# Twenty of forty-eight gate projections moved into a stage of their own, with seven block products for eight

## The chip, the cores and the metric

The kernel runs on one core of a Trainium2 chip. The metric is device time in microseconds (us) of one execution. Three executions of the kernel before took 2284.29 us in the median (2282.69 to 2284.61). On this core TensorE (PE in the profile) multiplies matrices, VectorE (DVE), ScalarE (ACT) and GpSimd (POOL) do everything else, and SyncE (SP) issues every DMA of this kernel. Each engine takes its instructions in the order written for it and waits at the first one whose operands aren't ready.

## The reference

One decoder layer on 1024 tokens of width 1024. Only its first part matters here:

```
proj = x @ w_in + b_in                     # 1024 x 8200
ml_qk, ml_v, ml_o, ml_if, da_q, da_k, da_v, gates = split(proj)
q, k = split(silu(causal_dwconv(ml_qk)))   # 4 heads of 128
h    = head_layer_norm(mlstm_chunkwise(q, k, ml_v, ...))
y_a  = (sigmoid(ml_o) * h) @ w_proj_a
o    = head_rms_norm(diff_attention(rope(da_q), rope(da_k), da_v))   # 8 heads
y_b  = o @ w_proj_b
g_a, g_b = split(sigmoid(gates))           # 1024 each
x = layer_norm(alpha * x + (g_a * y_a + g_b * y_b) @ w_mix_out)
```

After it come cross-attention into 256 memory tokens (its keys and values don't depend on x) and a SwiGLU feed-forward part. The columns `ml_o` (1024, eight blocks of 128) and `gates` (2048, sixteen blocks) are the 24 gate projections this case is about; with the blocks of `ml_qk`, `da_q` and `da_k` there are 48 blocks in `wfm`.

## The kernel before, in words

Every projection is done in float32 accuracy as three matmuls on split operands: a value is held as a rounded high part and a remainder (`whi`/`wlo` for weights, `bh`/`bl` for the input x, `to_hi` and `to_lo`), and `mm3` (L151 to L152) adds hi*hi, hi*lo and lo*hi in PSUM. The high part of a weight is made by ScalarE and GpSimd in turn (L139, L141), the remainder by VectorE three times of four and by GpSimd the fourth (L149).

`g_fm` (L191) projects one block of 128 columns: 8 blocks of 128 input channels by two halves of 512 tokens, so 2 x 8 x 3 = 48 matmuls of 128x512. It yields after every `mm3` by three matmuls; such a step is called a quantum here. `Weave` holds a queue of such generators. The mixers yield a number, and the driver then takes so many quanta from the queue (`W.pump(n)`); what is left is drained at fixed places. PE's order is therefore the order in which the program is written out. The order on the other engines is set by a scheduler, with priorities raised for loads and splits of weights.

The stages, by time in the profile:

1. **kv stage** (0 to 59 us): 16 blocks of cross-attention keys and values (`g_kv`, matmuls of 128x256). Beside them `g_x` loads the eight slabs of x and splits them into `xT`, which stays until the end of attention.
2. **mLSTM** (59 to about 455 us): first `g_first` (values and gate logits), then the projections `q`, `k` and two `o` blocks of head 0. For each of four heads `mlstm(h)` then pumps 68 quanta of the queue between its own small matmuls. The queue holds the next head's v, q, k and two `o` blocks (32 + 16 + 16 + 16 + 16 quanta), and five gate blocks in the last head. What isn't pumped is drained before the next head. `mlstm` starts with `PE.transpose` of k (L440), ends with transposes of the normalized h (L501). k comes from `g_proj_qk` (L350 to L369): evacuation on ACT (L356), a causal convolution on DVE (L359, L361), tanh on ACT (L367), a scale on POOL (L368) and a product on DVE (L369).
3. **Attention** (455 to about 1100 us): eight heads. Before head 0 `addB(0)` projects V, Q and K; each head pumps 64 quanta. `FILL` says what a head's queue holds: `P` is the next head's Q, K (16 quanta each) and, for every second head, V for two heads (32), `G` a gate block (16), `q`/`v` products of cross-attention weights (8 each). `scores` makes the probabilities (DVE, ACT, POOL), `values` transposes them (L719, L722), splits them and multiplies by V. `Y` are the first products after attention; they need `hT`, which `h0` to `h3` load into the memory of `xT`.
4. **Merge, cross-attention, feed-forward** (1100 to 2283 us). Gates kept in DRAM (`g_d`) are read again by `gate` (L827). The feed-forward part multiplies 2x2 blocks with seven products for eight (`g_seven`).

Of the kernel before, what the change touches and what calls it, by code (L numbers as in the profile page):

```python
# [115 lines left out]
def hybrid_layer(ctx: ExitStack, tc: tile.TileContext, a: dict, out: bass.AP):  # L116
# [74 lines left out]
    def g_fm(wsrc, acts, evac, pool=None, w=None):  # L191

        w = w or split_all(load_w(wsrc, pool), 1024, pool)
# [48 lines left out]
    g_d = dr.tile([16, 128, 1024], F, name="g_d")  # L242
    row_d = dr.tile([2, 32, 128], F, name="row_d")
# [3 lines left out]
    xT = big4(xp, "big", 4)  # L247
    with tc.tile_pool(name="mp", bufs=1, reuse_waits="tile") as mp:
# [11 lines left out]
        def g_x(k):  # L260
            load_slab(xT, k, a["xT"][:, k, :])
            yield from ()
# [15 lines left out]
        for k in range(0, 8, 2):  # L278
            if k % 4 == 0:
                turn["plan"] = ("v", "v")  # L280
                first.append(split_w(w0[:, k * 128:k * 128 + 512], mp))
# [16 lines left out]
    ngate = cst.tile([128, 16], F, name="ngate")  # L298
    V.tensor_scalar(ngate, bfm[:, 32:48], -1.0, None, op0=OP.mult)
# [6 lines left out]
    V.memset(pio2, math.pi / 2)  # L306

# [25 lines left out]
    with tc.tile_pool(name="ap", bufs=1, reuse_waits="tile") as A:  # L333
        ltbig = A.tile([128, 128], F, name="ltbig")
        dma(ltbig, a["c_ltbig"])
        bhalf = A.tile([128, 48], F, name="bhalf")
        V.tensor_scalar(bhalf, bfm, 0.5, None, op0=OP.mult)
# [75 lines left out]
        def g_gate(i, pool, tag, bufs):  # L413
            def ev(j, acc):
                gt = pool.tile([128, 512], F, tag=tag, name="gt", bufs=bufs)
                if i < NG_A:
                    res["act2"] = S.activation(gt, acc, AF.Tanh, scale=0.5, bias=bhalf[:, 32 + i:33 + i]).ins
                elif i < 8:
                    S.activation(gt, acc, AF.Exp, scale=-1.0, bias=ngate[:, i:i + 1])
                else:  # L420
                    S.activation(gt, acc, AF.Identity, bias=bfm[:, 32 + i:33 + i])
                dma(g_d[i][:, j * 512:(j + 1) * 512], gt)
# [88 lines left out]
        def addA(h):  # L511
# [3 lines left out]
            for d in range(2):  # L515
                W.add(f"o{h}{d}", g_proj_o(h, d))
# [76 lines left out]
        for h in range(4):  # L593
# [11 lines left out]
    with tc.tile_pool(name="bp", bufs=1, reuse_waits="tile") as B:  # L605
# [187 lines left out]

        gates = iter(range(NG_A, 16))

# [32 lines left out]
        def gate(i, pool, tag):  # L828
            gt = pool.tile([128, 1024], F, tag=tag, name="gt", bufs=2)
            dma(gt, g_d[i])  # L830
            if NG_A <= i < 8:
                S.activation(gt, gt, AF.Ln, bias=1.0)
                S.activation(gt, gt, AF.Exp, scale=-1.0)
                return gt
            if i >= 8:
                S.activation(gt, gt, AF.Tanh, scale=0.5)
# [11 lines left out]
        def add_fill(nm, h):  # L848
            if nm == "G":
                W.add("g", g_gate(next(gates), B, "rope", NROPE))  # L850
            elif nm == "P":
# [11 lines left out]
        add_fill("G", 0)  # L863
# [565 lines left out]
```

## Time and profile before

| | |
|---|---|
| median of three executions | 2284.29 us |
| profiled execution, its own time | 2285.06 us |
| its span (first to last instruction) | 2283.3 us |
| PE busy | 2207.3 us, 97% of the span |
| PE weight loads (PEld) | 2008.0 us, 88% |
| DVE / ACT / POOL busy | 1421.2 / 696.4 / 704.9 us |
| mean granted clock of PE | 0.989 of full speed |

PE's busy time in the profile comes from modelled ends: matmuls overlap, so one that follows another starts 0.227 us after it (128x512) though it is shown 0.39 us long. What PE really does is read from the starts and from the idle time in front of an instruction, with the engine that ended it.

### The profile page before, as it was taken

Reading aid. Unit: us, or ns where it says so; the run is one execution under the profiler, and the core shown is the slowest. Engines: PE = TensorE matmul, PEld = TensorE weight load, DVE = VectorE, ACT = ScalarE, POOL = GpSimd, SP = SyncE. Lnnn points to the kernel's source line nnn. Section 1 sums busy time; section 2 is a strip of 40 time slices with the busy share of each in tenths; the row PEclk is TensorE's granted clock in tenths of the full one; section 3 lists DMA queues with packets and bytes.
Section 4 is the critical chain, followed back from the end, with each engine's and each line's share of the span. In section 5 each row is a group of like instructions: output and inputs, shape, how many; then the busy total and the mean of one; then the engine's idle time right before and its main releaser. Section 6 shows DMA issues by size and latency. Waiting matters only on the chain.

```text
span 2283.3 us, 36224 instructions
## 1 busy us (share of the span) xinstructions
PE 2207.3 (97%) x14109; PEld 2008.0 (88%) x14109; DVE 1421.2 (62%) x2655; ACT 696.4 (30%) x1375; POOL 704.9 (31%) x720
## 2 busy tenths in 40 slices
PE   8999999999999999998999999997999999999997
PEld 8898898887988888886888999997899999999996
DVE  8536645357777676676535486478756665556657
ACT  3322213234454454445232123222211111111122
POOL 7124323233333332334412232245421111111124
PEclk9999999999999999999999999999999999999999
DMA  8322222344263343439733423222211111111122
GB/s 319 102 73 93 83 65 88 127 124 132 63 181 100 81 128 83 108 103 316 254 137 138 177 83 105 81 84 74 65 39 54 47 46 56 56 48 45 56 64 94
DMA packets 97963, 238.47 MB, mean 104 GB/s; under 512 B 12128, under 2 KB 30464, under 8 KB 97792
## 3 DMA queue, kind: packets, MB, share of 16 engines
q1 hardware_dynamic: 97792, 236.16, 32.5%
q8 instruction: 111, 1.82, 0.3%
q14 instruction: 60, 0.49, 0.1%
HBM read 168.92 MB, written 41.98 MB: 92 GB/s over the span
## 4 chain that ended last, share of the span: by engine, by line
PE 51%; DVE 5%; DMA 2%; issue 2%; POOL 1%; ACT 1%; SPq 0%; DVEq 0%; POOLq 0%; ACTq 0%
PE acc L152 32%; PE xb L152 7%; PE xa L152 5%; PE xc L152 5%; DVE wlo L149 1%; DMA vo_d<-ev 1%; PE sp L152 1%; DVE d L1040 1%; PE op L152 1%; DVE z L930 0%; DVE xb L149 0%; PE tp L722 0%; DVE z L926 0%; DVE u L1040 0%; PE tp L1007 0%
## 5 line engine op out<-in xcount | busy, mean ns | idle before, releaser
L141 POOL TENSOR_SCALAR whi<-wraw 128x512 fp32r<-128x512 f32 (+1 forms) x250 | 180.0, 720 | 880.3 <-issue 355.6
L152 PE MATMUL acc<-bh,whi 128*128 128x512 f32 x1024 | 418.1, 408 | 0.4 <-ACT gtok L389 0.4
L149 DVE TENSOR_TENSOR wlo<-wraw,whi 128x512 fp32r<-128x512 f32 (+1 forms) x379 | 306.3, 813 | 160.8 <-ACT whi L139 121.1
L152 PE MATMUL acc<-bh,wlo 128*128 128x512 f32 x1024 | 402.2, 393 | 0.0
L152 PE MATMUL acc<-bl,whi 128*128 128x512 f32 x1024 | 402.0, 393 | 0.0
L139 ACT ACTIVATE whi<-wraw 128x512 fp32r<-128x512 f32 (+1 forms) x252 | 157.4, 626 | 550.9 <-PE acc L152 273.9
L152 PEld LDWEIGHTS acc<-bh,wlo 128*128 128x128 f32 x1024 | 193.6, 189 | 42.5
L152 PEld LDWEIGHTS acc<-bh,whi 128*128 128x128 f32 x1024 | 194.0, 189 | 33.4 <-ACT gtok L389 0.6
L152 PEld LDWEIGHTS acc<-bl,whi 128*128 128x128 f32 x1024 | 194.3, 190 | 32.3
L152 PE MATMUL acc<-whi,bh 128*128 128x256 f32 (+1 forms) x728 | 213.2, 293 | 0.2 <-DVE ev L149 0.2
L152 PE MATMUL acc<-whi,bl 128*128 128x256 f32 (+1 forms) x728 | 205.6, 282 | 0.0
L152 PE MATMUL acc<-wlo,bh 128*128 128x256 f32 (+1 forms) x728 | 205.4, 282 | 0.0
L152 PE MATMUL xb<-xe,whi 128*128 128x256 f32 x1008 | 183.8, 283 | 10.3 <-DVE u L1040 7.4
L149 POOL TENSOR_TENSOR wlo<-wraw,whi 128x512 fp32r<-128x512 f32 (+1 forms) x125 | 174.1, 1393 | 9.8
L152 PEld LDWEIGHTS xb<-xe,whi 128*128 128x128 f32 x1008 | 155.9, 190 | 10.9 <-issue 6.8
L152 PE MATMUL xb<-xe,wlo 128*128 128x256 f32 x504 | 142.5, 283 | 0.0
L152 PEld LDWEIGHTS acc<-whi,bh 128*128 128x128 f32 x728 | 138.7, 190 | 2.0 <-DVE ev L149 0.4
L152 PEld LDWEIGHTS acc<-wlo,bh 128*128 128x128 f32 x728 | 138.7, 190 | 1.6
L152 PEld LDWEIGHTS acc<-whi,bl 128*128 128x128 f32 x728 | 138.6, 190 | 0.0
L1250 DVE SCALAR_TENSOR_TENSOR z<-z,acc 128x512 f32<-128x512 f32 x144 | 98.2, 685 | 53.4 <-PE acc L152 51.8
L152 PE MATMUL xa<-xb,whi 128*128 128x256 f32 x672 | 125.5, 287 | 5.2 <-ACT u L1162 5.2
L152 PE MATMUL acc<-wlo,hidh 128*128 128x512 f32 x320 | 124.7, 390 | 1.4 <-DVE wlo L149 1.4
(315 smaller groups left out, 5205.1 us busy)
## 6 DMA issues: line engine op xcount, KB each, us to landing
wraw<-in_wfm_dram SPq DMA_DIRECT2D x48, 512.0 KB, 3.6
wraw<-in_wg_dram SPq DMA_DIRECT2D x24, 512.0 KB, 3.6
wraw<-in_wu_dram SPq DMA_DIRECT2D x24, 512.0 KB, 3.5
wraw<-in_wd_dram SPq DMA_DIRECT2D x22, 512.0 KB, 3.5
hT_d<-hp SPq DMA_DIRECT2D x16, 512.0 KB, 2.8
g_d<-gt SPq DMA_DIRECT2D x32, 256.0 KB, 2.3
K<-rot SPq DMA_DIRECT2D x64, 128.0 KB, 2.3
klo<-raw SPq DMA_DIRECT2D x64, 128.0 KB, 2.3
```

Of the source, the lines that this page charges most:

```text
L139: S.activation(dst, src, AF.Copy)
L141: G.tensor_scalar(dst, src, 1.0, 0.0, op0=OP.mult, op1=OP.add)
L149: (V if eng == "v" else G).tensor_tensor(dst, src, hi.bitcast(F), op=OP.subtract)
L152: PE.matmul(o, l, r, start=start, stop=stop, skip_group_check=True)
L1040: V.tensor_tensor(dst, x_, y_, op=op)
L1250: V.scalar_tensor_tensor(zs, zs, ALPHA if q == 0 else 1.0, acc, op0=OP.mult, op1=OP.add)
```

## The change

Eight `o` blocks and twelve of sixteen gate blocks leave the mixers' queues. They are computed in pairs, in a stage of their own between the kv stage and the mLSTM. A pair of blocks (2 x 128 columns) is seen as a 2x2 matrix of blocks, x as well; sums of the blocks are formed, and seven products of 12 matmuls (128x512) and five additions out of PSUM give what eight products gave. The sums of x (`xs`, four more split tiles) are formed in the kv stage by `g_x`, which now takes two slabs at a time. tanh is applied at once; the results go to DRAM (`o_d`, `g_d`), and `g_o` loads a block of `o_d` where a head's `o` was projected. The last mLSTM head keeps four gate blocks. In attention the `G` entries are gone and the products of cross-attention weights are spread otherwise. In the kv stage weights are split into the general pool (4 buffers instead of 6) and three raw buffers stand for four.

```diff
-X_AT = (3, 4, 6, 7, 9, 10, 12, 13)
+X_AT = (3, 6, 9, 12)
-NRAW = 4
+NRAW = 3
-NG_A = 5
-FILL = (("G", "q0", "P", "G"), ("P", "q1"), ("G", "q2", "P", "G"), ("P", "G"), ("G", "q3", "P", "G"), ("P", "G"),
-        ("G", "P", "G"), ("h0", "v0", "h1", "v1", "h2", "v2", "h3", "v3", "Y"))
+NG_A = 4
+FILL = (("q0", "P", "q1"), ("P",), ("q2", "P", "q3"), ("P",), ("v0", "P", "v1"), ("P",), ("v2", "P", "v3"),
+        ("h0", "h1", "h2", "h3", "Y"))
...
         def g_x(k):
-            load_slab(xT, k, a["xT"][:, k, :])
+            raw = [load_w(a["xT"][:, kk, :]) for kk in (k, k + 4)]
+            b11, b12, b21, b22 = (r[:, hs] for r in raw for hs in HALVES)
+            for kk, r in zip((k, k + 4), raw):
+                for h, hs in enumerate(HALVES):
+                    to_hi(xT[h][0][:, kk, :], r[:, hs], "s")
+                    to_lo(xT[h][1][:, kk, :], r[:, hs], xT[h][0][:, kk, :], "v")
+            def put_(n, src):
+                to_hi(xs[n][0][:, k, :], src, "s")
+                to_lo(xs[n][1][:, k, :], src, xs[n][0][:, k, :], "g")
+            V.tensor_tensor(b11, b12, b11, op=OP.subtract)
+            put_(0, b11)
+            V.tensor_tensor(b12, b22, b12, op=OP.subtract)
+            put_(2, b12)
+            V.tensor_tensor(b22, b22, b11, op=OP.subtract)
+            put_(1, b22)
+            V.tensor_tensor(b21, b21, b22, op=OP.subtract)
+            put_(3, b21)
...
+        def g_dense(t0, t1, evac):
+            w = sums7([load_w(a["wfm"][t_]) for t_ in (t0, t1)])
+            def prod(bank, b, start=False, stop=False):
+                for k in range(4):
+                    mm3(bank, cut(w[b], k * 128, k * 128 + 128), (xblk[b][0][k], xblk[b][1][k]),
+                        start and k == 0, stop and k == 3)
+                    yield
...
+        for h in range(4):
+            W.add("o", g_sig(8 + 2 * h, o_d[2 * h:2 * h + 2]))
+        for i in range(0, 16 - NG_A, 2):
+            W.add("g", g_sig(32 + i, g_d[i:i + 2]))
+        W.drain()
...
-        def g_proj_o(h, d):
-            t_ = 8 + h * 2 + d
+        def g_o(h, d):
             og = A.tile([128, 1024], F, tag="og", name="og", bufs=3)
-            def ev(j, acc):
-                res["act2"] = S.activation(og[:, j * 512:(j + 1) * 512], acc, AF.Tanh, scale=0.5,
-                                           bias=bhalf[:, t_:t_ + 1]).ins
-            yield from g_fm(a["wfm"][t_], xT, ev)
+            dma(og, o_d[2 * h + d])
             G.tensor_scalar(og, og, 0.5, 0.5, op0=OP.mult, op1=OP.add)
...
             else:
-                for i in range(NG_A):
-                    W.add(f"g{i}", g_gate(i, A, "th", 2))
+                for i in range(16 - NG_A, 16):
+                    W.add(f"g{i}", g_gate(i))
...
         addB(0)
-        add_fill("G", 0)
         W.drain()
```

On PE, at the end of an mLSTM head before, the third transposes of h (`sm<-ident,hn`) follow the last matmul of the next head's k, and the `o` projections (`acc<-bh,whi` and so on) come behind them:

```order
L152 MATMUL acc<-bh,whi 128x512
L152 MATMUL acc<-bl,whi 128x512
L152 MATMUL acc<-bh,wlo 128x512
L501 MATMUL sm<-ident,hn 128x128 x4
L152 MATMUL acc<-bh,whi 128x512
L152 MATMUL acc<-bl,whi 128x512
L152 MATMUL acc<-bh,wlo 128x512
```

In all 96 such matmuls stand between the last matmul of k and the transposes of that k (`sm<-ident,y`). On PE at the same place of the changed kernel:

```order
L152 MATMUL acc<-bl,whi 128x512
L152 MATMUL acc<-bh,wlo 128x512
L598 MATMUL sm<-ident,hn 128x128 x8
L537 MATMUL sm<-ident,y 128x128 x4
L152 MATMUL acc<-whi,bh 128x256
L152 MATMUL acc<-wlo,bh 128x256
```

The first two rows are the end of k's projection; only eight transposes of h now stand between it and the transposes of k.

On POOL, at the start of the kv stage before (`whi`/`wlo` are weights, `bh`/`bl` are x):

```order
L141 TENSOR_SCALAR whi<-wraw 128x512 x2
L149 TENSOR_TENSOR wlo<-wraw,whi 128x512
L141 TENSOR_SCALAR whi<-wraw 128x512
L141 TENSOR_SCALAR bh<-wraw 128x512
L149 TENSOR_TENSOR bl<-wraw,bh 128x512
L141 TENSOR_SCALAR whi<-wraw 128x512
L141 TENSOR_SCALAR bh<-wraw 128x512
```

And on POOL at the same place of the changed kernel (`t0l` to `t3l` are remainders of the sums of x):

```order
L141 TENSOR_SCALAR whi<-wraw 128x512
L149 TENSOR_TENSOR t0l<-wraw,t0h 128x512
L149 TENSOR_TENSOR t2l<-wraw,t2h 128x512
L141 TENSOR_SCALAR whi<-wraw 128x512
L149 TENSOR_TENSOR t1l<-wraw,t1h 128x512
L149 TENSOR_TENSOR wlo<-wraw,whi 128x512
L149 TENSOR_TENSOR t3l<-wraw,t3h 128x512
```

The high parts of x left POOL for ACT, and 16 subtractions for the sums came; DVE got the 4 remainders of x that POOL had, and 16 subtractions of blocks.

On PE, at the end of attention head 0 before, the last group of `values` alternates transposes of probabilities (`tp`) with quanta (`acc`):

```order
L152 MATMUL op<-ath,vl 128x128
L152 MATMUL acc<-bh,whi 128x512
L152 MATMUL acc<-bl,whi 128x512
L152 MATMUL acc<-bh,wlo 128x512
L152 MATMUL acc<-bh,whi 128x512
L152 MATMUL acc<-bl,whi 128x512
L152 MATMUL acc<-bh,wlo 128x512
L722 MATMUL tp<-ident,e_4941 128x128
L722 MATMUL tp<-ident,e_4990 128x128
```

On PE at the same place of the changed kernel, where the queue of head 0 has run out:

```order
L152 MATMUL op<-ath,vl 128x128
L819 MATMUL tp<-ident,e_5832 128x128
L819 MATMUL tp<-ident,e_5881 128x128
L819 MATMUL tp<-ident,e_5832 128x128
L819 MATMUL tp<-ident,e_5881 128x128
L819 MATMUL tp<-ident,e_5832 128x128
```

The quanta are gone from the last group of heads 0, 2, 4 and 6, whose queues hold 48 quanta for the 64 that are pumped.

## Rows read from the trace of the kernel before

**Rows 1.** The page: busy time, share and instructions of the engines.

```profile
PE 2207.3 (97%) x14109; PEld 2008.0 (88%) x14109; DVE 1421.2 (62%) x2655; ACT 696.4 (30%) x1375; POOL 704.9 (31%) x720
```

**Rows 2.** Windows by stage: length, PE, PEld, DVE, ACT, POOL, PEclk, DMA, GB/s.

```profile
10.00:55.00 45.00, 43.52 (x349) 42.84 (x349) 44.40 (x52) 17.68 (x37) 42.72 (x37) 1.00 0.96 346
125.00:450.00 325.00, 325.00 (x1833) 284.69 (x1832) 158.07 (x269) 86.56 (x186) 98.59 (x85) 1.00 0.26 88
500.00:1050.00 550.00, 524.82 (x3052) 461.03 (x3051) 391.92 (x973) 260.75 (x567) 193.72 (x210) 0.98 0.41 114
1050.00:1075.00 25.00, 17.21 (x69) 13.18 (x68) 14.46 (x33) 10.79 (x21) 8.22 (x9) 0.86 0.99 351
```

**Rows 3.** Chain of waits, a run of 128x512 matmuls: start, length, what.

```profile
1649.48 21.82 PE acc L152 x96
```

**Rows 4.** Groups by form, 10 to 55 us: busy, mean ns | idle before.

```profile
L149 DVE TENSOR_TENSOR wlo<-wraw,whi 128x512 fp32r<-128x512 f32 x23 | 25.2, 1126 | 0.0
...
L141 POOL TENSOR_SCALAR whi<-wraw 128x512 fp32r<-128x512 f32 x15 | 14.9, 998 | 10.9 <-DMA wraw<-in_wxk_dram 10.9
L149 DVE TENSOR_TENSOR bl<-wraw,bh 128x512 fp32r<-128x512 f32 x12 | 14.7, 1235 | 0.5 <-POOL bh L141 0.5
L149 POOL TENSOR_TENSOR wlo<-wraw,whi 128x512 fp32r<-128x512 f32 x7 | 11.3, 1620 | 0.6
...
L149 DVE TENSOR_TENSOR ev<-acc,ev 128x256 fp32r<-128x256 f32 x14 | 5.8, 413 | 0.1
```

**Rows 5.** Timeline of DVE before POOL begins: start, length, instruction.

```profile
3.79 0.69 DVE L149 TENSOR_TENSOR wlo<-wraw,whi 128x512 fp32r<-128x512 f32 x1
```

**Rows 6.** Timeline of PE at the end of mLSTM head 0.

```profile
186.11 0.60 PE L501 MATMUL sm<-ident,hn 128*128 128x128 f32 x4
...
208.82 0.60 PE L440 MATMUL sm<-ident,y 128*128 128x128 f32 x4
```

**Rows 7.** Timeline of ACT at the same place.

```profile
190.89 0.67 ACT L356 ACTIVATE pad<-acc,bfm 128x512 f32<-128x512 f32 x1
196.27 0.63 ACT L139 ACTIVATE hp<-hs 128x512 fp32r<-128x512 f32 x1 [4.71 <-DMA hT_d<-hp]
...
201.08 1.15 ACT L367 ACTIVATE th<-y 128x512 f32<-128x512 f32 x2 [0.31 <-DVE y L361]
```

**Rows 8.** Timeline of POOL at the same place.

```profile
192.04 3.03 POOL L149 TENSOR_TENSOR hp<-hs,hp 128x512 fp32r<-128x512 f32 x2
...
202.19 1.20 POOL L368 TENSOR_SCALAR th<-th 128x512 f32<-128x512 f32 x2
```

**Rows 9.** Timeline of DVE at the same place.

```profile
196.21 4.84 DVE L361 SCALAR_TENSOR_TENSOR y<-pad,cw,y 128x1024 f32<-128x1024 f32 x3
...
202.83 2.10 DVE L369 TENSOR_TENSOR y<-y,th 128x512 f32<-128x512 f32 x2 [1.66 <-POOL th L368]
```

**Rows 10.** Timeline of PE where mLSTM head 0 begins.

```profile
127.83 0.37 PE L591 MATMUL sm<-ident,gall 32*128 32x32 f32 x3
```

**Rows 11.** Timeline of POOL ahead of it.

```profile
116.41 2.40 POOL L431 TENSOR_TENSOR Mb<-Mb,ltbig 128x1024 f32<-128x1024 f32 x1 [6.37 <-DMA Mb<-row_d]
...
121.15 1.19 POOL L368 TENSOR_SCALAR th<-th 128x512 f32<-128x512 f32 x2
```

**Rows 12.** Timeline of DVE ahead of it.

```profile
121.80 2.11 DVE L369 TENSOR_TENSOR y<-y,th 128x512 f32<-128x512 f32 x2 [6.21 <-POOL th L368]
```

**Rows 13.** PE's waits in attention, 500 to 1050 us: total, times, longest.

```profile
PE tp L722 <- DVE e L693: 12.7, 7, 3.6
PE sp L152 <- DMA klo<-raw: 9.0, 7, 2.3
```

**Rows 14.** Timeline of PE late in attention's last head.

```profile
1068.43 0.79 PE L152 MATMUL acc<-whi,kvh 128*128 128x512 f32 x1 [6.37 <-ACT ev L765]
```

**Rows 15.** PE alone, windows behind two waits: length, busy, PEclk, DMA, GB/s.

```profile
552.00:555.00 3.00, 2.81 (x9) 0.51 0.02 5
...
1068.00:1074.00 6.00, 5.57 (x14) 0.52 1.05 378
```

More of the change, by code (lines that the diff above doesn't have):

```diff
@@ L191, in g_fm @@
     def g_fm(wsrc, acts, evac, pool=None, w=None):
-        w = w or split_all(load_w(wsrc, pool), 1024, pool)
+        w = w or split_all(load_w(wsrc, pool))
         for j, (ah, al) in enumerate(acts):
@@ L242, in hybrid_layer @@
     g_d = dr.tile([16, 128, 1024], F, name="g_d")
+    o_d = dr.tile([8, 128, 1024], F, name="o_d")
     row_d = dr.tile([2, 32, 128], F, name="row_d")
@@ L247, in hybrid_layer @@
     xT = big4(xp, "big", 4)
+    t_stack = ExitStack()
+    tp_ = t_stack.enter_context(tc.tile_pool(name="tpool", bufs=1, reuse_waits="tile"))
+    xs = [(tp_.tile([128, 4, 512], R, name=f"t{i}h"), tp_.tile([128, 4, 512], R, name=f"t{i}l")) for i in range(4)]
     with tc.tile_pool(name="mp", bufs=1, reuse_waits="tile") as mp:
@@ L280, in hybrid_layer @@
                 turn["plan"] = ("v", "v")
-                first.append(split_w(w0[:, k * 128:k * 128 + 512], mp))
+                first.append(split_w(w0[:, k * 128:k * 128 + 512]))
                 turn["plan"] = None
@@ L297, in hybrid_layer @@
     dma(bfm, a["b_fm"])
-    ngate = cst.tile([128, 16], F, name="ngate")
-    V.tensor_scalar(ngate, bfm[:, 32:48], -1.0, None, op0=OP.mult)
     dag = cst.tile([128, 8], F, name="dag")
@@ L308, in hybrid_layer @@
+    t_stack.close()
     nlam = cst.tile([128, 1], F, name="nlam")
@@ L335, in hybrid_layer @@
         dma(ltbig, a["c_ltbig"])
-        bhalf = A.tile([128, 48], F, name="bhalf")
-        V.tensor_scalar(bhalf, bfm, 0.5, None, op0=OP.mult)
         cw = A.tile([128, 32], F, name="cw")
@@ L400, in g_proj_v, with g_gate @@
             res["v", h] = v
-        def g_proj_o(h, d):
-            t_ = 8 + h * 2 + d
+        def g_o(h, d):
             og = A.tile([128, 1024], F, tag="og", name="og", bufs=3)
-            def ev(j, acc):
-                res["act2"] = S.activation(og[:, j * 512:(j + 1) * 512], acc, AF.Tanh, scale=0.5,
-                                           bias=bhalf[:, t_:t_ + 1]).ins
-            yield from g_fm(a["wfm"][t_], xT, ev)
+            dma(og, o_d[2 * h + d])
             G.tensor_scalar(og, og, 0.5, 0.5, op0=OP.mult, op1=OP.add)
             res["o", h, d] = og
-        def g_gate(i, pool, tag, bufs):
+            yield from ()
+        def g_gate(i):
             def ev(j, acc):
[L415 to L421, printed above, removed]
+                gt = A.tile([128, 512], F, tag="th", name="gt", bufs=2)
+                res["act2"] = S.activation(gt, acc, AF.Tanh, scale=0.5, bias=bhalf[:, 32 + i:33 + i]).ins
                 dma(g_d[i][:, j * 512:(j + 1) * 512], gt)
@@ L515, in addA @@
             for d in range(2):
-                W.add(f"o{h}{d}", g_proj_o(h, d))
+                W.add(f"o{h}{d}", g_o(h, d))
         addA(0)
@@ L792, in g_vo @@
                     spill(acc, vo_d[2 * cb:2 * cb + 2, :, 2 * h + kt, :].rearrange("b p c -> p b c"))
-        gates = iter(range(NG_A, 16))
         def attention():
@@ L830, in gate @@
             dma(gt, g_d[i])
[L831 to L836, printed above, removed]
             G.tensor_scalar(gt, gt, 0.5, 0.5, op0=OP.mult, op1=OP.add)
@@ L848, in add_fill @@
         def add_fill(nm, h):
-            if nm == "G":
-                W.add("g", g_gate(next(gates), B, "rope", NROPE))
-            elif nm == "P":
+            if nm == "P":
                 addB(h + 1)
```

59 lines of the change are left out of this document (added).

## The prediction

> **What bounds the kernel now.** I read the page first: PE is busy for 97% of the span, no other engine for more than 62% [rows 1]. That share says only that PE is the engine to look at; where it is really full is seen in the windows by stage [rows 2]. From 125 to 450 us, in the mLSTM, PE is busy for 325.00 of 325 us and nothing ever ends a wait of it: whatever the other engines do there lies beside matmuls. In attention, 500 to 1050 us, it idles for 25.2 of 550 us at a DVE busy for 71%. In the kv stage DVE and POOL are both full (44.40 and 42.72 of 45 us) and PE still keeps up. So the path is PE's own work in nearly every stage, and a matmul taken away shortens the run by its start-to-start time, as long as what it covered stays covered. That last condition is what this case turns on, so the next views are those of who waits for whom at the places where work is taken out: the end of an mLSTM head on four engines [rows 6 to 9], the start of head 0 [rows 10 to 12], PE's waits in attention [rows 13], its last head [rows 14].
>
> **The saving.** Twenty blocks of 48 matmuls (960) become ten pairs of 7 x 12 (840). The price of one is read from the chain of waits: 96 matmuls of 128x512 in 21.82 us, 0.2273 us each [rows 3]. 120 x 0.2273 = 27.3 us less. The moved matmuls themselves cost the same in the new stage; there they need per pair five additions out of PSUM and seven splits, which fit beside 84 x 0.2273 = 19.1 us of PE.
>
> **The kv stage.** By the order, POOL's large instructions go from 25 high parts and 12 remainders to 15 and 23, and DVE's from 41 two-operand instructions of 128x512 to 61 (25 remainders of weights, 4 of the memory, 16 of x, 16 differences), beside 16 `ev`. A remainder takes POOL 1.62 us and a high part 1.00 us [rows 4]: 15 x 1.00 + 23 x 1.62 = 52 us of POOL for some 43. A remainder takes DVE 1.13 to 1.24 us here [rows 4], and 0.69 us while POOL stands still [rows 5], so the two engines hinder each other. At the pace of before DVE does 38 such instructions in 45 us beside a full POOL (35 in the rows, 3 of the memory), so 44 in 52 us; the other 17 then take 17 x 0.69 = 12 us. POOL starts after 10 us, so the sums of x are whole at about 10 + 52 + 12 = 74 us, where PE left this stage at 59 us: 15 us, and 1 us for the first pair's sums, which follow in DVE's queue. Bounds: 3 us (all 61 at 0.69 us, POOL alone sets the end at 62 us) and 28 us (all 61 at 1.15 us plus 16 x 0.41 us, 77 us). I take 16, near POOL's full rows.
>
> What the Trainium skill says of this, in "SBUF — State Buffer", section "Who interferes with whom": a DVE instruction with two SBUF inputs and a GpSimd instruction that reads SBUF exclude each other, "it's an exclusive lock". By that rule alone the old stage would have taken the sum, 38 x 0.69 + 42.7 = 69 us, where the trace has 45; the direction agrees, the size does not. By the rule the new stage would need 61 x 0.69 + 52 = 94 us from 10 us on, 30 us more than the sum here takes.
>
> **The mLSTM's heads.** Before, the last matmul of the next head's k ends at 186.11 us, and 96 matmuls of `o` follow until the transposes of k at 208.82 us, which wait for nothing [rows 6]. In that time k passes through the other engines: evacuation at 190.89 us, behind `hp` on ACT [rows 7], the convolution until 201.05 us, tanh from 201.08 us, the scale on POOL from 202.19 us behind the remainders of `hp` [rows 8], the product; its first half is there at about 203.9 us [rows 9]. That is 17.8 us after PE let go of it. In the changed kernel only eight transposes (0.7 us) stand in between, and everything behind the transposes of k on PE, the next head's whole queue included, waits with them. Upper bound of the wait: 17.1 us, the time of before. Lower: the chain by itself, 0.67 + 0.8 + 3 x 1.29 + 0.6 + 0.6 + 0.9 = 7.4, less 0.7: 6.7 us. The changed order still has `hp` ahead of the evacuation on ACT, and `wib`, a weight's split, `hp` and `og` ahead of the scale on POOL; so I take 15 us, near the rows, for heads 1 to 3: 45 us. At head 0 the last matmul of k ends 96 x 0.2273 = 21.8 us ahead of 127.83 us [rows 3, 10], at 106.0 us. Its scale sits on POOL behind `Mb`, which waits for a DMA until 116.41 us, and `wib` [rows 11]; the first half of k is there at about 122.9 us [rows 12], and POOL's order there has not changed. That is 16.6 us less a little: 16 us. Sum of the four 61 us, bounds 27 and 67 us.
>
> After a wait PE is granted the lower of its two clock levels for a while, 0.51 and 0.52 of 2.4 GHz in the windows behind a wait of 2.7 us and of 6.4 us [rows 14, 15], where it lost some 1.4 and 2.6 us. Four new long waits at 2 us: 8 us (0 to 11).
>
> **Attention.** Head 0 loses the gate block that stood behind its first K: 2 us, what PE waited at other heads for `klo` [rows 13]. Heads 0, 2, 4 and 6 keep 48 quanta for 64 pumped, so the last group of values runs bare. 16 quanta of 3 x 0.2273 us are 10.9 us of cover per head. DVE's 71% of a head of 74.9 us (the first scores of heads 0 and 7 are 524 us apart) is 53 us, some 51 without the gate blocks; PE has 48 quanta and some 20 us of the head's own there, 54 us, so DVE is nearly as long as PE and its lag shows. Already with cover PE waited seven times for the probabilities, 12.7 us [rows 13]. I take 5 us a head, 20 us; bounds 0 and 44. Heads 1, 3 and 5 keep all their 64 quanta and stay as they are. In the last head `v0` to `v3` ran together with the 8 MB of `hT`, at a DMA share of 0.99 [rows 2], and PE waited 6.37 us for an evacuation held up by them [rows 14]; now these products run in heads 4 and 6: 8 us less with the clock's loss, bounds 0 and 12. The gates' removed steps in the merge and the DMA round trips of `o_d` and `g_d` I cost at nothing: PE is full there, and a block is stored a head or more before it is read.
>
> **Sum.** -27.3 + 16 + 61 + 8 + 2 + 20 - 8 = +71.7 us on the profiled execution's own 2285.06 us, which is 0.8 us above the median of the runs: 2356 us.
>
> **Rivals.**
> - *k comes sooner.* With the splits of `o` gone the queues ahead of k are shorter, and heads 1 to 3 wait 6.7 us, head 0 12 us; the clock then costs 5 us: -27.3 + 16 + 32 + 5 + 22 - 8 = +39.7, 2325 us. For it: DVE is half idle in this stage. Against it: `hp` waits 4.71 us for a DMA [rows 7], which no shorter queue changes.
> - *k is covered*, the other side. If the transposes of k find it ready, because its chain runs ahead of the transposes of h, then the four waits and the clock go: 71.7 - 61 - 8 = +2.7, 2288 us, no difference that can be told; and with the kv stage at its lower bound 13 us less, 2275 us. It decides below 2 us for all four waits together. Against it: k's last matmul is eight transposes ahead in PE's order, and its bare chain alone takes 7.4 us.
> - *Attention's even heads are bound by DVE*: the whole 10.9 us show, 24 us more, 2380 us. For it: 51 of 54 us; against it: the half of the group's wait that the other heads cover.
> - *DVE and POOL exclude each other more than they did* in the kv stage, because POOL now runs mostly two-operand instructions: 30 us more, 2386 us.
> - *The new stage isn't bound by PE* and a pair takes as long as eight products: the 27.3 us don't come, 2384 us. Against it: the feed-forward part runs the same scheme with PE full.
>
> **How the numbers follow.** Forecast 0.51, k sooner 0.18, even heads 0.12, exclusion 0.08, k covered 0.06, new stage 0.05. A change under 0.2%, 4.6 us, can't be told from none. Slower by more: all but the covered k and a tail of the sooner one, 0.93; within 0.2%: 0.04; faster: 0.03. The range goes from 2310 us (the sooner k with the lower costs of attention) to 2390 us (two of the upper bounds at a time don't fit, one does).
>
> **What would show it.** In the profile of the changed kernel PE's waits name DVE's product of k or the transposes of `y` at four places, some 15 us each, with PEclk near 0.5 behind them; the first matmul of the new stage starts at about 74 us, and that stage lasts about 191 us with PE full. Transposes of `e` wait at the end of every second head. The 6 us wait in the last head is gone. If PE is full between the heads of the mLSTM, the forecast is wrong in its largest term.

## The result: slower by 6.4%, twice what was forecast

The changed kernel takes 2431.4 us (median of four, 2429.69 to 2434.95) against 2284.45 us of the kernel before, run beside it: a ratio of 1.064 with a 95% interval of 1.0615 to 1.0665. The forecast was 2356 us with a range of 2310 to 2390 us; the sign was right and the size was not. The page of the changed kernel, against [rows 1]:

```profile
PE 2220.8 (91%) x13989; PEld 2016.0 (83%) x13989; DVE 1505.3 (62%) x2787; ACT 704.9 (29%) x1403; POOL 728.5 (30%) x749
```

TensorE has its 120 matmuls less and is shown busy for 13.5 us more, since matmuls behind a wait run at the lower clock; its share falls from 97% to 91%. Where the time went shows when both traces are cut at the same events: the end of the kv products, the first transposes of `k` in mLSTM head 0 and in the last head, the first scores of attention's head 0 and head 7. First the windows of the kernel before (columns as in [rows 2]), then those of the changed one:

```profile
0.00:59.10 59.10, 49.07 (x386) 48.10 (x387) 49.07 (x63) 22.49 (x45) 43.55 (x41) 1.00 0.89 313
59.10:128.10 69.00, 67.77 (x390) 59.18 (x388) 37.83 (x64) 22.67 (x43) 19.79 (x21) 1.00 0.32 107
128.10:370.30 242.20, 242.20 (x1407) 214.17 (x1406) 129.00 (x212) 65.23 (x146) 80.63 (x68) 1.00 0.23 77
370.30:497.80 127.50, 127.50 (x673) 109.90 (x672) 49.01 (x93) 32.53 (x60) 29.02 (x27) 1.00 0.39 118
497.80:1022.20 524.40, 501.64 (x2938) 441.87 (x2937) 372.46 (x915) 244.79 (x527) 181.88 (x195) 0.98 0.39 107
1022.20:2283.30 1261.10, 1219.17 (x8325) 1134.80 (x8323) 783.83 (x1309) 308.68 (x556) 350.02 (x371) 0.99 0.29 97
```

```profile
0.00:80.00 80.00, 55.26 (x385) 51.93 (x386) 70.11 (x82) 35.96 (x68) 49.50 (x42) 0.96 0.68 225
80.00:343.70 263.70, 240.54 (x1135) 200.78 (x1134) 134.49 (x205) 77.21 (x131) 68.18 (x77) 0.96 0.35 116
343.70:578.10 234.40, 182.35 (x1117) 165.91 (x1117) 120.47 (x203) 53.06 (x120) 67.72 (x58) 0.89 0.23 77
578.10:685.90 107.80, 107.80 (x588) 94.41 (x589) 41.45 (x87) 27.56 (x53) 23.14 (x21) 0.98 0.32 100
685.90:1203.10 517.20, 446.06 (x2587) 392.67 (x2586) 369.47 (x916) 239.43 (x523) 182.96 (x192) 0.94 0.44 119
1203.10:2427.90 1224.80, 1188.76 (x8185) 1110.33 (x8183) 769.30 (x1296) 271.65 (x509) 337.00 (x361) 0.99 0.26 88
```

In each window the difference in TensorE's instructions, times 0.2273 us [rows 3], is the matmul work that came or went (the moved ones have 512 columns but for 28 of 256 columns that left attention's window, 24 of them for the one before it; such a one starts 0.12 us after another in both traces, and is counted so); what is left over is waiting and clock. The last column is the forecast's share of that remainder.

| stage | length, us | matmul work, us | waiting and clock, us | forecast, us |
|---|---|---|---|---|
| kv products | +20.9 | 0 | +20.9 | +16 |
| dense stage and the way to head 0's `k` | +194.7 | +169.3 | +25.4 | +18 |
| mLSTM heads 0 to 2, up to the last head's `k` | -7.8 | -65.9 | +58.1 | +51 |
| last mLSTM head, Q, K, V of attention's head 0 | -19.7 | -21.7 | +2.0 | 0 |
| attention, seven heads | -7.2 | -77.0 | +69.8 | +22 |
| attention's last head and all that follows | -36.3 | -31.8 | -4.5 | -8 |
| sum | +144.6 | -27.1 | +171.7 | +99 |

The count of matmuls came out as forecast, and their price in the new stage too: the second to the tenth pair start 19.03 to 19.25 us one after another, where 19.1 us were taken. The last mLSTM head and what follows attention's seven heads came out near their forecast, kv is 5 us over, the dense stage and the mLSTM's heads 7 us each, and attention 48 us: 77 us of matmuls left its seven heads, and they are 7.2 us shorter.

TensorE's waits from 282 to 690 us in the changed kernel (engine, line, what it waited for: total, times, longest), and two of its instructions around the start of one mLSTM head (start, length, instruction, idle time before it):

```profile
PE sm L537 <- DVE y L475: 67.8, 4, 17.4
```

```profile
481.35 1.03 PE L598 MATMUL sm<-ident,hn 128*128 128x128 f32 x8
499.77 1.11 PE L537 MATMUL sm<-ident,y 128*128 128x128 f32 x4 [17.38 <-DVE y L475]
```

These are the four waits that the prediction named, for the product of `k` behind its convolution. Where 96 matmuls stood before the transposes of `k` [rows 6], eight transposes stand now. What DVE and then POOL do in such a wait:

```profile
484.62 1.40 DVE L601 SCALAR_TENSOR_TENSOR hs<-sm,mlg,og 128x512 f32<-128x512 f32 x2
485.94 1.73 DVE L465 TENSOR_SCALAR y<-pad,cw,cb 128x1024 f32<-128x1024 f32 x1
490.75 0.75 DVE L601 SCALAR_TENSOR_TENSOR hs<-sm,mlg,og 128x512 f32<-128x512 f32 x1 [3.07 <-POOL hp L149]
491.41 5.82 DVE L467 SCALAR_TENSOR_TENSOR y<-pad,cw,y 128x1024 f32<-128x1024 f32 x3
...
498.63 1.69 DVE L475 TENSOR_TENSOR y<-y,th 128x512 f32<-128x512 f32 x2 [1.27 <-POOL th L474]
```

```profile
484.78 2.35 POOL L529 TENSOR_TENSOR wib<-wib,y 128x1024 f32<-128x1024 f32 x1 [0.63 <-DVE y L475]
...
489.45 2.49 POOL L149 TENSOR_TENSOR hp<-hs,hp 128x512 fp32r<-128x512 f32 x2
```

The convolution of `k` stands in the middle. `k` was evacuated at 482.9 us, but the convolution starts at 485.94 us, behind the product of `q` and two `hs`, the old head's result. Between its first step and the other three DVE idles 3.07 us for the next `hs`, whose buffer POOL's remainder `hp` frees, and that stands behind `wib` and a weight's split. The steps themselves take 1.73 and 5.82 us, where they take 0.81 and 3.92 us in the kernel with the order alone, below. These make up most of the step from the 7 us of the bare chain to 17.4 us.

In attention the changed kernel's TensorE waits as follows (685.9 to 1281 us), against [rows 13]:

```profile
PE tp L819 <- DVE e L790: 19.6, 10, 3.6
PE acc L152 <- ACT raw L720: 19.5, 4, 5.0
PE acc L152 <- ACT ev L862: 15.4, 4, 4.2
PE op L152 <- DVE atl L149: 14.4, 16, 2.5
PE acc L152 <- DMA bh<-hT_d: 3.6, 1, 3.6
```

The waits have no one cause by name: TensorE arrives early in several places, at the probabilities of DVE, at accumulators that ACT has yet to empty, at the remainders of the transposes. The 6.37 us wait of the last head [rows 14] is gone; a 3.6 us wait for the loads of `hT` has come in its place.

### The profile page after: what moved, and what is told of

Read it like the earlier page. It is cut to its first block, busy times and chain, and to the rows that moved or that the text cites. A ratio compares the mean times of both kernels' runs of the same rounds, so it can differ in the third digit from the quotient of the medians.

```text
span 2427.9 us, 36331 instructions
## 1 busy us (share of the span) xinstructions
PE 2220.8 (91%) x13989; PEld 2016.0 (83%) x13989; DVE 1505.3 (62%) x2787; ACT 704.9 (29%) x1403; POOL 728.5 (30%) x749
## 3 DMA queue, kind: packets, MB, share of 16 engines
q1 hardware_dynamic: 101248, 244.55, 31.9%
## 4 chain that ended last, share of the span: by engine, by line
PE 71%; DVE 13%; issue 6%; POOL 4%; DMA 4%; ACT 2%; SPq 1%; POOLq 0%; DVEq 0%; ACTq 0%
PE acc L152 40%; PE xb L152 10%; PE xc L152 7%; PE xa L152 7%; PE sp L152 2%; DVE wlo L149 1%; PE op L152 1%; DVE y L467 1%; PE nm L152 1%; DVE z L1016 1%; ACT e L785 1%; DVE e L790 1%; POOL wlo L149 1%; DVE e L779 1%; DVE raw L722 1%
## 5 line engine op out<-in xcount | busy, mean ns | idle before, releaser
L149 DVE TENSOR_TENSOR wlo<-wraw,whi 128x512 fp32r<-128x512 f32 (+1 forms) x394 | 294.7, 751 | 118.2 <-ACT whi L139 83.6
L139 ACT ACTIVATE whi<-wraw 128x512 fp32r<-128x512 f32 (+1 forms) x262 | 163.9, 626 | 645.7 <-PE acc L152 277.3
L152 PE MATMUL acc<-bh,whi 128*128 128x512 f32 x704 | 293.3, 417 | 3.9 <-DMA bh<-hT_d 3.6
L152 PE MATMUL acc<-bl,whi 128*128 128x512 f32 x704 | 279.3, 397 | 0.6 <-DMA bl<-hT_d 0.6
L152 PE MATMUL acc<-bh,wlo 128*128 128x512 f32 x704 | 279.8, 397 | 0.0
L149 POOL TENSOR_TENSOR wlo<-wraw,whi 128x512 fp32r<-128x512 f32 (+1 forms) x130 | 179.5, 1381 | 10.0
L152 PEld LDWEIGHTS acc<-bh,wlo 128*128 128x128 f32 x704 | 134.7, 191 | 30.0
L152 PEld LDWEIGHTS acc<-bh,whi 128*128 128x128 f32 x704 | 135.6, 193 | 26.0 <-DMA bh<-hT_d 3.9
L152 PEld LDWEIGHTS acc<-bl,whi 128*128 128x128 f32 x704 | 135.5, 192 | 22.7 <-DMA bl<-hT_d 1.1
L1336 DVE SCALAR_TENSOR_TENSOR z<-z,acc 128x512 f32<-128x512 f32 x144 | 98.4, 686 | 53.7 <-PE acc L152 52.2
```

The costliest lines, as they stand in the source:

```text
L139: S.activation(dst, src, AF.Copy)
L149: (V if eng == "v" else G).tensor_tensor(dst, src, hi.bitcast(F), op=OP.subtract)
L152: PE.matmul(o, l, r, start=start, stop=stop, skip_group_check=True)
L1336: V.scalar_tensor_tensor(zs, zs, ALPHA if q == 0 else 1.0, acc, op0=OP.mult, op1=OP.add)
```

## The experiments

The kernel before, run beside them, took 2285.4, 2287.6 or 2286.8 us in the median, so a difference of some 3 us between two runs at different times says little.

**The values between `k` and its use.**

```
-            W.add(f"v{h}", g_proj_v(h) if h else g_first())
+            if h == 0:
+                W.add("v0", g_first())
             W.add(f"q{h}", g_proj_qk(h, 0))
             W.add(f"k{h}", g_proj_qk(h, 1))
+            if h:
+                W.add(f"v{h}", g_proj_v(h))
```

> The changed kernel with the next head's projections queued as q, k, v instead of v, q, k (head 0 keeps its values first), so that v's 192 matmuls of 128x256, about 23 us, stand on TensorE between k's projection and the transposes of k. Theory (the lag of k's chain is what the heads wait for): the waits of 17.5 us at heads 1 to 3 go, with about 1.5 us of clock each, 57 us less, 2374 us; head 0's 15.9 us stays. Rival (k is held by what stands ahead of its scale on GpSimd, whatever its place on TensorE): a wait of 10 us or more stays at each head, 2410 to 2431 us. Rival (v is late in its turn): the waits come back at the first products with v, 2395 us or more.

2372.3 us, 59.1 us less than the changed kernel (ratio to before 1.0377, 1.0347 to 1.0407). TensorE goes from the old head's transposes to those of the next `k` without a pause, and of the four waits the one of head 0 is left:

```profile
402.04 1.03 PE L598 MATMUL sm<-ident,hn 128*128 128x128 f32 x8
402.91 0.60 PE L537 MATMUL sm<-ident,y 128*128 128x128 f32 x4
```

```profile
PE sm L537 <- DVE y L475: 15.1, 1, 15.1
```

Three waits of 17.4 us are 52 us. Most of the other 7 us is the clock: the first hundred matmuls behind each of the changed kernel's four waits take 1.5 to 2.1 us longer than the same hundred in the kernel before, where no wait precedes them. At these three heads the lag of `k` was the cause, and other work of TensorE's in front of its use is the whole cure.

**One part of the change alone: `o` ahead of `k`, in the kernel before.**

```
+            for d in range(2):
+                W.add(f"o{h}{d}", g_proj_o(h, d))
             W.add(f"q{h}", g_proj_qk(h, 0))
             W.add(f"k{h}", g_proj_qk(h, 1))
-            for d in range(2):
-                W.add(f"o{h}{d}", g_proj_o(h, d))
```

> The kernel before with one part of the change alone: the two o projections of an mLSTM head stand ahead of q and k instead of behind k, so that the transposes of k follow k's projection directly; no dense stage, no work less. Theory (the lag of k's chain was covered by the o projections): four waits of 15 to 17.5 us and some 1.5 us of clock each, 2285 + 68 + 6 = about 2359 us. Rival (the waits come with the loads of the stored o and the emptier queues of the changed kernel): under 5 us each, 2305 us or less.

2345.0 us against 2287.6 us beside it, ratio 1.0255 (1.0235 to 1.0276): the order alone costs 57 us. The waits are four, 46.8 us in all, and shorter than in the changed kernel:

```profile
331.06 0.69 PE L440 MATMUL sm<-ident,y 128*128 128x128 f32 x2 [12.04 <-DVE y L369]
```

Here `hs` and `hp` of the old head do not fall into the convolution of `k`, and 12 us is what its chain takes beside the weights' splits and `wib`. So some 5 us of the changed kernel's 17.4 us go with the old head's end, which now meets this chain; that is read from the two traces, and no run tests it by itself.

**The block sums of x left out.** The four products that want a sum take a block of x; the matmuls and the weights' sums stay.

```
-            V.tensor_tensor(b11, b12, b11, op=OP.subtract)
-            put_(0, b11)
...
-        xblk += [[[x_[:, k, :] for k in range(4)] for x_ in xs[n]] for n in range(4)]
+        xblk += [xblk[n] for n in (0, 1, 2, 1)]
```

> The changed kernel without the block sums of x: the kv stage splits x alone, and the four products of a pair that want a sum take a block of x in its place (this computes something else; the number of matmuls and of the weights' sums stays). Theory (the sums' differences and remainders on VectorE and GpSimd are what delays TensorE there): the first product of the dense stage starts at about 60 us as the kv stage ended before, not at 79.9 us, and its first pair waits less; 20 to 28 us less, 2403 to 2411 us. Rival (the smaller buffers of the kv stage, three of x and of weights for four, and weights out of the shared pool, are a cost of their own): the stage still ends after 66 us, and the time is 2415 us or more.

2406.9 us, 24.5 us less than the changed kernel. The kv products end at 59.2 us as before, with the smaller buffers:

```profile
0.00:59.20 59.20, 49.24 (x385) 48.14 (x386) 42.89 (x66) 27.34 (x52) 22.20 (x26) 1.00 0.94 323
```

So the 20.9 us of the kv stage go with the sums, all of them. The first pair still waits, 2.9 us for a high part on POOL among others: its weights' sums are a chain that nothing covers.

**The sums behind the kv stage.** x is loaded a second time, and two gates are done plainly ahead of nine dense pairs.

```
+        for i in range(2):
+            W.add("g", g_plain(i))
+            for k in range(2 * i, 2 * i + 2):
+                W.add("xs", g_xs(k))
```

> The changed kernel with the sums taken out of the kv stage: x is loaded a second time behind it, and the sums are made beside two gate projections done plainly (2 x 10.9 us) ahead of the dense stage, which keeps nine pairs; TensorE has 12 matmuls more, 2.7 us. Theory (TensorE can cover the sums, they were only at a place where VectorE is full): the kv stage ends at 59 to 62 us, the nine pairs start at about 83 us and no wait of more than 3 us stands between; 2431 - 32 + 2.7 + 3 = about 2405 us. Rival (the sums take longer than the cover, GpSimd's sixteen remainders alone are 25 us, and the first pair's weights queue behind them): a wait of 8 us or more ahead of the first pair's second product, 2413 us or more.

2419.4 us: 12 us less, not 26. The kv stage ended at 59.0 us, but the first dense product started at 90.9 us, 31.9 us later, for 21.8 us of plain gates: there is a wait of 2.5 us among the gates and one of 6.9 us for a high part ahead of that product. The rival's time came, with its wait one product earlier than it said. x's second load shared three buffers with the weights here; the second of the mended kernels below gives it its own, and these two waits are gone.

**The gates back in attention.** Only the eight `o` projections are in the dense stage; the gates and their place are those of the kernel before.

```
-        for i in range(0, 16 - NG_A, 2):
-            W.add("g", g_sig(32 + i, g_d[i:i + 2]))
...
-FILL = (("q0", "P", "q1"), ("P",), ("q2", "P", "q3"), ("P",), ("v0", "P", "v1"), ("P",), ("v2", "P", "v3"),
-        ("h0", "h1", "h2", "h3", "Y"))
+FILL = (("G", "q0", "P", "G"), ("P", "q1"), ("G", "q2", "P", "G"), ("P", "G"), ("G", "q3", "P", "G"), ("P", "G"),
+        ("G", "P", "G"), ("h0", "v0", "h1", "v1", "h2", "v2", "h3", "v3", "Y"))
```

> The changed kernel with only the eight o projections in the dense stage (4 pairs); all sixteen gates are done as in the kernel before (5 in the last mLSTM head, 11 as fill in attention, products of the values in the last head). Theory (attention lost its cover): from the first scores of head 0 to those of head 7 the time is again about 524 us with some 25 us of idle; TensorE has 72 matmuls more, 16 us, in all; attention gives back about 68 us: 2431 + 16 - 68 = 2379 us. Rival (the attention is slower for another reason, such as the projections that went through DRAM or the kv stage): idle time of attention stays above 80 us, and the time is 2431 us or more.

2384.8 us (ratio 1.0432, 1.0402 to 1.0462), 47 us less although TensorE has 16.4 us more to do. The sum over the seven heads' windows:

```profile
sum 524.10, PE 500.81 PEld 440.94 DVE 371.99 ACT 244.71 POOL 181.08; mean PE 71.54 PEld 62.99 DVE 53.14 ACT 34.96 POOL 25.87
```

524.10 us, and 524.40 us in the kernel before: attention's share of the loss comes from its own fill alone and from nothing that the earlier stages leave behind. Against the changed kernel the seven heads do 351 instructions more, 77 us of matmuls, and are 6.9 us longer.

**The gates' matmuls thinned out, in the kernel before.** Of the eleven gates in attention one step of eight is done; loads, splits, evacuations and the count of steps stay.

```
                 for k in range(KT):
+                    if k == 0:
+                        mm3(acc, cut(w[0], 0, 128), (ah[:, 0, :], al[:, 0, :]), True, True)
                     yield
```

> The kernel before, with the eleven gates that fill attention cut to one of their eight steps along the contraction (42 of 48 matmuls left out each, their loads, splits and evacuations stay, and the pump counts the empty steps; it computes something else): 462 x 0.2273 us = 105 us of TensorE less, ten blocks of it between the first scores of heads 0 and 7. Theory (attention's heads have a floor near 70 us and the gates' matmuls were nearly free there): the seven heads go from 524 us to 485 to 500 us, the time to 2240 to 2255 us, so that two thirds of the removed work bring nothing. Rival (attention is bound by TensorE, as my sum took it): 524 - 95 = 429 us there, and about 2185 us.

2258.4 us against 2286.8 us beside it, ratio 0.9876 (0.9848 to 0.9904). 105 us of matmuls are gone and the run is 28 us shorter. The first two heads and the sum of the seven:

```profile
485.80:557.90 72.10, 59.53 (x305) 50.34 (x306) 56.02 (x130) 35.76 (x76) 27.59 (x29) 0.90 0.53 150
557.90:629.80 71.90, 71.19 (x465) 65.71 (x465) 52.30 (x136) 33.59 (x76) 23.64 (x27) 0.96 0.30 80
...
sum 506.30, PE 445.19 PEld 390.47 DVE 375.18 ACT 243.97 POOL 183.50; mean PE 63.60 PEld 55.78 DVE 53.60 ACT 34.85 POOL 26.21
```

The seven heads lost 373 matmuls, 84.8 us, and became 18.1 us shorter, less than the 24 to 39 us that even this expectation gave them. Head 0 lost 65 instructions and took 72.1 us where it had taken 71.6 us. Heads 2, 4 and 6 became 6.3 to 7.6 us shorter; heads 3 and 5 lost 41 and 42 instructions and became 1.6 and 0.8 us longer, though TensorE had been busy for 76.94 of 77.5 us in head 3 before. So the eleven gates were cheap where they stood, about 2.6 us each in the mean for 9.5 us of matmuls taken out, and this is the number that the prediction lacked.

**The query and value products out of the even heads.** `z` is eight empty quanta.

```
-FILL = (("q0", "P", "q1"), ("P",), ("q2", "P", "q3"), ("P",), ("v0", "P", "v1"), ("P",), ("v2", "P", "v3"),
-        ("h0", "h1", "h2", "h3", "Y"))
+FILL = (("z", "P", "z"), ("P",), ("z", "P", "z"), ("P",), ("z", "P", "z"), ("P",), ("z", "P", "z"),
+        ("q0", "h0", "q1", "v0", "q2", "h1", "q3", "v1", "h2", "v2", "h3", "v3", "Y"))
```

> The changed kernel with the query and value products (q0 to q3, v0 to v3, 8 times about 11.5 us of TensorE) taken out of the even attention heads and all put into the last one; in their place the pump counts 8 empty quanta each. Theory (a head of attention has a floor of about 72 us, set by the way of its rows through VectorE and ScalarE, and fill below it is free): the four even heads lose 23 us of matmuls each and still take 68 to 74 us, so the time grows by most of 92 us, to 2500 us or more. Rival (waits are a fixed price that comes on top of the matmuls): the heads shorten by 23 us each to about 51 us, and the time stays at about 2431 us. Between the two, each even head says how much of it was hidden.

2450.0 us, 18.6 us more. A size in the expectation was wrong: such a product is 48 matmuls of 256 columns or 24 of 512, 5.5 to 5.8 us, so 45 us moved in all, not 92. The even heads took 67.0 to 69.2 us where they had taken 73.5 to 74.5, and the odd ones 69.9 to 71.5:

```profile
687.40:756.60 69.20, 55.05 (x268) 47.19 (x269) 47.38 (x122) 27.88 (x61) 19.47 (x21) 0.83 0.41 97
756.60:828.10 71.50, 66.26 (x422) 59.34 (x421) 52.55 (x133) 32.83 (x75) 23.51 (x26) 0.98 0.21 58
...
sum 484.00, PE 413.91 PEld 362.32 DVE 352.18 ACT 214.67 POOL 156.09; mean PE 59.13 PEld 51.76 DVE 50.31 ACT 30.67 POOL 22.30
```

Neither theory holds as it stood. A head with nothing but the next head's projections for fill still needs 67 to 69 us; but of these 45 us 33 came out of the heads, far more than of the gates' matmuls. The products took their splits and evacuations with them, 17 us of DVE, 25 us of ACT and 27 us of POOL over the seven heads, which the thinned gates had left in place. That the heads follow these engines rather than TensorE is a reading that fits both runs; no run takes the splits and evacuations out and leaves the matmuls, so which engine or chain sets a head's time stays open.

**Their evacuation on DVE.**

```
-            S.activation(e, acc, AF.Copy)
+            V.tensor_copy(e, acc)
```

> The changed kernel with the evacuation of the query and value products (q0 to q3, v0 to v3: 32 copies of 128x512) on VectorE instead of ScalarE. Theory (kind of fill: these products want an accumulator every two quanta, and ScalarE frees it only behind the exponentials that wait for VectorE): the waits of the even heads for ScalarE's evacuations, 34.9 us in all, shrink to under 10 us, the time is about 2400 us. Rival (amount of fill: TensorE only waits there instead of later): these waits move to the transposes of e, the heads stay at 74 us and the time within 5 us of 2431 us. Rival (VectorE sets the attention's pace): the copies, 32 x 0.7 = 22 us, make it slower, 2445 us.

2436.5 us, 5 us more; the ratios to the kernel before, 1.0658 and 1.0640, can't be told apart. TensorE's longest waits in the seven heads, and their sum:

```profile
PE acc L152 <- DVE ev L862: 27.7, 6, 6.7
PE tp L819 <- DVE e L790: 19.7, 8, 3.6
PE acc L152 <- ACT raw L720: 19.6, 4, 5.2
```

```profile
sum 527.20, PE 448.41 PEld 395.38 DVE 388.72 ACT 224.58 POOL 178.91; mean PE 448.41 PEld 395.38 DVE 388.72 ACT 224.58 POOL 178.91
```

The theory of the slow ScalarE fell: the waits for `ev` only changed the engine, from 15.4 to 27.7 us, and the heads became 10 us longer in the trace for 19 us more on DVE and 15 us less on ACT. ScalarE's name behind the wait did not make it the cause.

**Three kernels meant to mend it.** The first has four dense pairs for `o`, the sums behind kv beside two plain gates, `q, k, v`, two gates behind head 0's `k`, four in the last mLSTM head and eight in attention.

> Dense stage for the eight o projections only (four pairs, 48 matmuls or 10.9 us less than before); sums of x made behind the kv stage beside two plain gate projections; q, k, v as the order of a head's projections; two gates behind k of head 0, four in head 3, eight as fill in the even attention heads (none in heads 3 and 5, which had 75.5 us of matmuls before). Theory (each loss has the cause named: 4 pairs gain 10.9 us, the kv stage costs 5 to 8 us, the mLSTM waits are gone, and the heads 3 and 5 of attention shorten by some 15 us as the two gates leave): 2285 - 10.9 + 7 - 15 - 2 = about 2264 us. Rival (attention's heads 3 and 5 lose cover and stay at 77 us): 2280 us. Rival (the sums have no cover that suffices): 2290 us or more.

2302.8 us, ratio 1.0069 (1.0052 to 1.0086). No wait is left at the `k` of any head, and heads 0 to 2 take 59.0 us each with TensorE full. But 2264 us were expected: the three gates that left attention's fill cost their 10.9 us each outside, and the 48 matmuls that left the seven heads, 10.9 us, shortened them by 3.4 us, to 521.0 us. The second puts them back as fill and gives the sums six buffers of their own.

```
-            raw = [load_w(a["xT"][:, kk, :]) for kk in (k, k + 4)]
+            raw = [Dn.tile([128, 1024], F, tag="xr", name="xr", bufs=6) for _ in range(2)]
```

> As the kernel with all mended, but all eleven gates of attention stand there as fill again (as in the kernel before), one gate is left in mLSTM head 3, and the second load of x for the sums has six buffers of its own instead of the weights' three. Dense stage: the eight o projections, four pairs. Against that kernel three gates, 32.7 us, leave the stages where TensorE is full, and attention is as long as before, 12 us more. Theory (a gate as fill in attention is nearly free, and one outside costs its 10.9 us): 2303 - 33 + 12 - 3 for the sums' waits = about 2279 us. Rival (head 3 of the mLSTM needs its fill; with one gate for four its own chain shows): 10 to 20 us more, 2290 to 2300 us.

2304.9 us, ratio 1.0082 (1.0058 to 1.0105), where 2279 us were expected. The two plain gates now run in 21.8 us without a wait; the first pair pays instead, as the sums aren't there yet. TensorE's waits up to 130 us:

```profile
PE xb L152 <- ACT t1h L139: 8.0, 2, 4.2
...
PE xb L152 <- POOL t1l L149: 3.7, 2, 2.4
```

4.4 us of a wait for `hn` in the last mLSTM head, left with one gate, come on top. The third does head 0's `o` plainly and has three pairs.

> As the one above, but the two o projections of mLSTM head 0 are done plainly behind k of head 0 (they cover its lag), so that the dense stage has three pairs and head 3 keeps three gates; two plain gates stand ahead of the dense stage. TensorE has 12 matmuls, 2.7 us, more than above. Theory (cover is enough everywhere): 2282 us. Rival (head 3 needed its fill): faster than the one above by more than 5 us.

2312.0 us, ratio 1.0111 (1.0091 to 1.0131): 7 us more than the second where 3 us were expected. It waits as long for `t1`, 11.7 us, so a pair less saves no wait. But that is not where the 7 us are: by the traces it reaches attention 5.8 us sooner than the second, and then takes 531.4 us for 523.5 us in the seven heads and 1269.9 us for 1263.1 us behind them, for the same work; no run says why. None of the three beats the kernel before. Four pairs save 10.9 us; in the second kernel the way to the `k` of head 0 is 120.4 us longer than in the kernel before for 433 matmuls, 98.4 us, and these 22 us, the first pair's waits for the sums and the clock behind them above all, take that and more.

## Why the prediction went wrong

**The saving** was right: 120 matmuls less, and pairs of 84 at 19.03 to 19.25 us. The rival of a new stage that isn't bound by TensorE fell with that.

**The mLSTM's heads** were right in place, mechanism and nearly in size: 61 us and 8 us of clock forecast, four waits of 67.8 us found, just above the upper bound of 67 us; the clock, 1.5 to 2.1 us a wait, makes 7.5 us. Both kernels that change only the order (59 us back, 57 us lost) show it from either side. The rival that `k` comes sooner fell: the queues ahead of `k` still held the old head's `hs` and `hp`, which the kernel with the order alone did not have there.

**The kv stage** was mis-sized by 5 us. The step that failed is that POOL would be full for 52 us and then done, so that DVE's last 17 two-operand instructions run at 0.69 us. In the changed kernel's kv stage (groups by form: busy, mean ns) DVE got no faster:

```profile
L149 DVE TENSOR_TENSOR wlo<-wraw,whi 128x512 fp32r<-128x512 f32 x26 | 27.2, 1066 | 2.5 <-ACT whi L139 1.1 <-POOL whi L141 0.8 <-PE acc L152 0.5
L149 DVE TENSOR_TENSOR bl<-wraw,bh 128x512 fp32r<-128x512 f32 x16 | 15.5, 1012 | 0.0
...
L279 DVE TENSOR_TENSOR wraw<-wraw 128x512 f32<-128x512 f32 x4 | 5.9, 1472 | 0.0
```

DVE was busy for 70.1 of 80 us. Its 62 such instructions took 1.10 us in the mean, and so did the 41 of the kernel before. One by one, 28 of the 62 took 0.68 to 0.69 us and the others 0.98 to 1.79 us, with fast and slow ones mixed from start to end. POOL's 49.5 us came as forecast, but with gaps in between, in which it waited for high parts from ACT and for loads, among others; its last remainder ends at 78.0 us. The rival of the exclusion, another 30 us, did not come true.

**The dense stage** was bound by TensorE but for its start: it waits 4.22 us and 1.08 us for the first pair's weights, where 1 us was taken (within the 16 us of kv). With the clock behind them the first pair takes 27.6 us, 8.5 us more than the others. The wait at head 0's `k` is 15.7 us, and what is left of the stage's 25.4 us is a wait of 1.5 us.

**Attention** is where the forecast fell, 48 of the 73 us that were missing. The step that failed is the first one, "a matmul taken away shortens the run by its start-to-start time", with its condition, "as long as what it covered stays covered". It was read from TensorE's busy share, 524.82 of 550 us [rows 2], and that row does not bear it: in a stage where TensorE idles 25 us with cover, the matmuls may be the cover themselves. So the sum credited the gates in full and charged 5 us a head for a bare group, 20 us. Measured, the thinned gates gave back a fifth of their matmuls inside the seven heads. 77 us less work there, with a fifth returned, would be 61 us; 69.8 us were found as waiting and clock. The rival of the even heads looked for the right kind of loss, a lag that fill had covered, in too small a place: it asked only for the bare last group, 10.9 us a head, and took the odd heads as unchanged, though they too lost matmuls; that DVE binds these heads, as it says, is not shown. Heads 0 and 1 of the changed kernel show how little the matmuls set the time there:

```profile
685.90:759.90 74.00, 59.97 (x342) 53.54 (x341) 50.89 (x127) 34.01 (x73) 25.51 (x27) 0.93 0.56 150
759.90:834.30 74.40, 69.83 (x446) 63.25 (x445) 54.47 (x136) 34.61 (x78) 26.09 (x28) 0.95 0.27 73
```

The second does 104 matmuls of 256 columns more, 12.5 us, in 0.4 us more. The trace of before had a weaker hint, in the windows of its heads 0, 1 and 3:

```profile
497.80:569.40 71.60, 67.01 (x370) 57.51 (x369) 51.23 (x125) 34.19 (x74) 25.57 (x27) 0.98 0.43 124
569.40:641.30 71.90, 71.22 (x477) 65.47 (x476) 53.27 (x136) 34.43 (x78) 24.86 (x28) 1.00 0.28 75
...
716.00:793.50 77.50, 76.94 (x489) 69.39 (x488) 55.99 (x138) 35.72 (x78) 24.64 (x29) 1.00 0.31 84
```

Head 1 does 107 instructions more than head 0 in the same time. By columns they are 60 of 512 less and 168 of 256 more, so 6.5 us of work. Heads 3 and 5, with 489 instructions each and 12 us more work than head 0, took 77.5 and 81.6 us, so there the time did follow in part. The prediction did not compare heads with each other, and so had no price for the gates but that of their starts.

**The last head's 8 us** came as 4.5 us over all that follows the seven heads; the loads of `hT` are still late for their first user.

## What to carry to other kernels

Before work is moved out of a stage, ask what the stage would take without it: compare units of the stage that hold different amounts of it, by their matmuls' starts and not by their number (here heads that differ by 12.5 us of matmuls and by 0.4 us of time), or take the matmuls out and leave the rest. If the time doesn't follow, that work is filling, and where TensorE is full it costs its full time (here 19.1 us a pair). A projection that stands behind another one in the order may be there for the lag of the one ahead; move it and the next consumer on that engine waits, unless something else of that length takes its place.

## What was not expected of the hardware

- With 373 matmuls, 84.8 us, less in seven heads, the heads took 18.1 us less, while the granted clock of a head fell from between 0.95 and 1.00 to between 0.87 and 0.96; part of what a thinner TensorE could give is lost at the lower of its levels. Behind a 17.4 us wait of the changed kernel it was 0.50:

```profile
499.80:502.00 2.20, 2.20 (x11) 2.20 (x12) 0.52 (x1) 1.08 (x4) 1.04 (x1) 0.50 0.81 294
```

- Two-operand instructions of DVE that write over one of their operands were hindered beside POOL no less than the others: the four groups of differences in the kv stage have means of 1.05 to 1.47 us, the remainders of weights and of x 1.07 and 1.01 us, and the first two differences of the first mended kernel took 0.68 and 0.69 us with POOL at rest. The Trainium skill, "SBUF — State Buffer", section "Who interferes with whom", calls that an exclusive lock; in the kv stage DVE's 70.1 and POOL's 49.5 us of busy time lie in 80 us, so by the busy times of the trace the two overlap, and the direction alone agrees; how much of each busy time is waiting no view here shows.
